# Two directions of a recurrence on different halves of the PSUM partitions

## The chip, the core and the metric

The kernel runs on one core of a Trainium2 chip. The metric is the device time of one execution in microseconds. Three executions of the kernel before took 3052.81, 3056.64 and 3072.35 us, a median of 3056.64 us.

The engines are called by the profile's names: PE is TensorE's matmul unit, PEld its loads of stationary operands, DVE is VectorE, ACT is ScalarE, POOL is GpSimd, SP issues the DMAs.

## The reference

Two layers over 256 context tokens and 256 latent tokens, 1024 channels wide. A layer projects its normalised input with one wide matrix, feeds three token mixers (a bidirectional RWKV-7, a bidirectional gated linear recurrence, a neighbourhood attention), merges them by gates, and ends with a gated MLP. The change touches the RWKV-7 mixer alone, whose heart is this scan, run for 16 heads, forwards and backwards:

```python
def step(S, inp):
    r_t, w_t, k_t, v_t, kk_t, a_t = inp
    sa = jnp.einsum('bhvk,bhk->bhv', S, -kk_t)
    S = (S * w_t[:, :, None, :] + sa[..., None] * (kk_t * a_t)[:, :, None, :]
         + v_t[..., None] * k_t[:, :, None, :])
    return S, jnp.einsum('bhvk,bhk->bhv', S, r_t)
```

S is a 64x64 state for each head. The context goes first, and its last state begins the latent tokens' scan; the outputs of the two directions are added.

## The kernel before, in words

**Layout.** Channels lie on the 128 partitions, the 512 tokens (context, then latent) along the free dimension. The big products (the input projection, tiles `pj`; the MLP, `fg`, `fu`, `fo`; the merges) go through `mm3` (L240): each weight tile is split into a high and a low part (`wh` on ACT, L225; `wl` on DVE or POOL, L228), and three matmuls of 128x128 weights with 512 tokens (256 for latent tokens alone) stand for one product. There are thousands of them, and they fill PE wherever nothing else is due.

**The recurrence in chunks.** A pair of heads takes 128 channels, so a layer has 8 pairs. The scan of a pair is done in 8 chunks of 64 tokens. What lies within a chunk is solved by products and a triangular inverse beforehand: `rw_gram` (L571), `rw_inv` (L632, a chain of some 62 small DVE instructions, tiles `itmp` and `AT`) and `rw_inv2` (L671). What goes from chunk to chunk is `rw_seq` (L697). It has two directions d and two heads h, so every step is four products of 64 output columns, for (d, h) = (0,0), (0,1), (1,0), (1,1), the list `dh`. For each chunk i:

- `r` (L720): G times [state; values], into PSUM partitions 64 to 127. ACT copies all four to `r1` (L724).
- `yp` with `RT` (L726 to L728, through `ymm`, L710): the old state's part of the outputs. Its stationary operand lies on 64 partitions, that of `r` on 128.
- POOL scales the old state by its decay into `sg` (L732).
- `sa` (L735): the inverse times `r1`, into PSUM partitions 0 to 63. ACT copies the four, negated, to SV (L737).
- `sp` (L741): the state's update, into PSUM partitions 0 to 63. DVE adds it to `sg` and writes the next state into SV (L745; L747 where there is no `sg`).
- `yp` with `Gm` (L748 to L750, through L710): the rest of the outputs.

An output product `yp` of chunk c goes to partitions 0 to 63 where c is even and to 64 to 127 where it is odd; the two directions take their chunks in opposite order, so within a step their halves differ.

These products are fp32, and each is two records of LDWEIGHTS and two of MATMUL in the trace: 8 records for a step of four.

**What sets the order.** The program is traced part by part for each pair (the string `order` in the table CFG, L54 and L104; `T` is `rw_seq`), each part with a priority. A list scheduler works out, from the dependences, its own costs and these priorities, the order in which every engine takes its instructions. On the chip each engine keeps to its order, and PE waits at a product whose operand is late even if a projection behind it is ready.

Of the kernel before, what the change touches and what calls it, by code (L numbers as in the profile page):

```python
# [10 lines left out]
F32 = mybir.dt.float32  # L11
F32R = mybir.dt.float32r
AF = mybir.ActivationFunctionType
ALU = mybir.AluOpType
AX = mybir.AxisListType
PSUM = bass.MemoryType.PSUM
# [3 lines left out]
P = 128  # L20
# [31 lines left out]
# per layer: the order in which a head pair's parts are traced, their priorities, how the products of the other  # L52
# mixers are spread beside them, and which engine takes the work that several could take
# [104 lines left out]
class Net:  # L158
# [51 lines left out]
    # ---- weights: raw -> (hi, lo) in float32r  # L210
    def phase(self, l, name, wps=None):
        """From here on the weights rotate among wps; where their low parts are worked out: 1 for GpSimd."""
        self.lo, self.wn = CFG[l]["lo"][name], 0
        if wps:
            self.wps, self.wi = wps, 0
# [49 lines left out]
    # ---- rms statistics of the tokens a ... b - 1: acc holds the sums of squares over the channel tiles  # L265
# [15 lines left out]
    def stat(self, st, sq, a, b, first, last):  # L281
        """Adds the sums of sq over its channels to st, a column for 128 tokens."""
# [13 lines left out]
    # ---- conditioning vectors of a layer: mod[128, 48, 2]  # L296
# [16 lines left out]
    def ada_chunk(self, l, n, kind="c"):  # L313
        """Columns 512 n ... 512 n + 511 of the modulation, four column groups side by side on TensorE."""
# [22 lines left out]
        # modulation: h = x rstd (ng (1 + sc)) + sh ; x += (g ng) o rstd  # L337
# [12 lines left out]
    def layer_consts(self, l):  # L350
# [19 lines left out]
        # softplus(-lam) = max(-lam, 0) + log1p(exp(-|lam|)); log1p(u) = 2 atanh(u / (2 + u))  # L370
# [53 lines left out]
    # ---- A: RWKV-7  # L424
# [16 lines left out]
    def rw_start(self, Q):  # L441
# [4 lines left out]
        # stacked over the partitions: (hi, lo) of w, (lo, hi) of a  # L446
# [14 lines left out]
    def rw_key(self, R, Q, p, n0):  # L461
# [15 lines left out]
        # normalised key  # L477
# [93 lines left out]
    def rw_gram(self, R, u, n0):  # L571
        nc = self.nc
        KR, BK = u["KR"], u["BK"]
        G = R.tile([P, 2, 2, 2, NCH, 64], F32, tag="Gm", name="Gm")  # part, d, h, c
# [22 lines left out]
    def rw_rows(self, R, u, n0):  # L597
# [3 lines left out]
        # from here on [beta; k] decayed to the end of its chunk  # L601
# [3 lines left out]
        # value rows by token, for both directions  # L605
# [12 lines left out]
        # rows by token of [beta; k]  # L618
# [13 lines left out]
    def rw_inv(self, R, u):  # L632
# [9 lines left out]
        if self.cfg['f1']:  # L642
            # the block beside them makes room for the rows of keys
# [10 lines left out]
        # columns s of the inverse: rows 0-63 hold the odd ones, rows 64-127 the even ones, both in the even places  # L654
# [16 lines left out]
    def rw_inv2(self, R, u):  # L671
# [4 lines left out]
        T1 = Ap  # rows 0-31: T11, rows 96-127: Q  # L676
# [20 lines left out]
    def rw_seq(self, R, u, n0):  # L697
# [16 lines left out]
        for i in range(NCH):  # L714
            cs = (i, STEP1[i])
            gcb = gC[:, :, :, i:i + 1].rearrange("p d h o -> p (d h) o").to_broadcast([64, 4, 64])
            S0 = SV[0:64, i].rearrange("p d h v -> p (d h) v")
            pr = self.ps("q", "r1").rearrange("p (x v) -> p x v", v=64)
            for d, h in dh:
                nc.tensor.matmul(pr[64:128, 2 * d + h], lhsT=G[:, 0, d, h, cs[d], :], rhs=SV[:, i, d, h, :],  # L720
                                 start=True, stop=True)
            rs = R.tile([P, 4, 64], F32, tag="r1", name="r1")
            r1 = rs[64:128]
            nc.scalar.activation(r1, pr[64:128, 0:4], AF.Copy)  # L724
# [9 lines left out]
            for d, h in dh:  # L734
                nc.tensor.matmul(pa[0:64, 2 * d + h], lhsT=TT[:, d, h, cs[d], :], rhs=r1[:, 2 * d + h, :],  # L735
                                 start=True, stop=True)
            nc.scalar.activation(S0, pa[0:64, 0:4], AF.Copy, scale=-1.0)  # L737
            if i < NCH - 1:
                pp = self.ps("q", "sp").rearrange("p (x v) -> p x v", v=64)
                for d, h in dh:  # L740
                    nc.tensor.matmul(pp[0:64, 2 * d + h], lhsT=Bt[:, d, cs[d], 64 * h:64 * h + 64],  # L741
                                     rhs=SV[:, i, d, h, :], start=True, stop=True)
                S1 = SV[0:64, i + 1].rearrange("p d h v -> p (d h) v")
                if sg is not None:
                    nc.vector.tensor_tensor(S1, pp[0:64, 0:4], sg, op=ALU.add)  # L745
                else:
                    nc.vector.tensor_copy(S1, pp[0:64, 0:4])  # L747
# [847 lines left out]
```

## Time and profile before

| | |
|---|---|
| times of three runs | 3052.81, 3056.64, 3072.35 us |
| profiled execution: its own time from the first to the last instruction (its span) | 3050.6 us |
| PE busy | 2886.2 us, 95% |
| DVE busy | 1968.9 us, 65% |
| ACT busy | 1411.1 us, 46% |
| POOL busy | 840.6 us, 28% |
| mean granted TensorE clock | 0.959 |

No time of the profiled execution beyond its span is listed. A matmul's end is modelled in this profile: a projection matmul is shown with 0.39 us and the next one starts 0.23 us after it. So what a product costs PE is read from the starts of the matmuls around it, not from busy time.

### The profile page before, as it was taken

What the parts mean: (1) busy time and instruction counts of PE and PEld (TensorE: products, weight loads), DVE (VectorE), ACT (ScalarE), POOL (GpSimd) and SP (SyncE); (2) the same over time, 40 slices, a digit from 0 to 9 for tenths busy, and PEclk for the clock granted to TensorE, in tenths of its full rate; (3) what the DMA queues carried; (4) which work ended last, traced back from release to release, by engine and by line L of the source; (5) the groups of instructions that cost most, each with busy time, mean ns of one, the idle gap of its engine ahead of it and who ended that gap; (6) DMA issues with size and microseconds to landing.
All of it is one profiled execution on the core that took longest, in us unless ns stands there. A gap on an engine that the chain in (4) does not pass through costs nothing. (4 is left out here: it accounts for less than half of the span.)

```text
span 3050.6 us, 53179 instructions
## 1 busy us (share of the span) xinstructions
PE 2886.2 (95%) x21104; PEld 2265.9 (74%) x21104; DVE 1968.9 (65%) x3745; ACT 1411.1 (46%) x2485; POOL 840.6 (28%) x788
## 2 busy tenths in 40 slices
PE   7999999999999999999999998998999999998998
PEld 5666776766767678687778886776776777788898
DVE  6757658576686653465444267788677778775784
ACT  4454455554455452253323245454554545554553
POOL 3341322424234225100000113433432433414220
PEclk9999999999999899998999998998988999999899
DMA  6222122211222225755562352222222122245653
GB/s 229 81 70 67 59 71 66 74 60 56 69 76 70 84 100 180 273 190 180 198 223 92 107 183 82 62 78 69 68 72 69 62 70 78 77 140 205 222 188 115
DMA packets 130553, 344.39 MB, mean 113 GB/s; under 512 B 14720, under 2 KB 41600, under 8 KB 130304
## 3 DMA queue, kind: packets, MB, share of 16 engines
q1 hardware_dynamic: 123392, 334.69, 33.1%
q10 hardware_dynamic: 6912, 6.29, 0.7%
q8 instruction: 166, 2.72, 0.4%
q14 instruction: 83, 0.68, 0.1%
HBM read 301.08 MB, written 25.17 MB: 107 GB/s over the span
## 5 line engine op out<-in xcount | busy, mean ns | idle before, releaser
L225 ACT ACTIVATE wh<-wr 128x1024 fp32r<-128x1024 f32 (+1 forms) x402 | 420.8, 1048 | 581.0 <-PE pj L247 209.1
L248 PE MATMUL pj<-hh,wl 128*128 128x512 f32 (+1 forms) x1440 | 559.0, 389 | 41.4 <-DVE wl L228 40.0
L246 PE MATMUL pj<-hh,wh 128*128 128x512 f32 (+1 forms) x1440 | 569.7, 397 | 5.8 <-ACT gt L1088 3.0
L228 DVE TENSOR_TENSOR wl<-wr,wh 128x1024 fp32r<-128x1024 f32 (+1 forms) x310 | 398.2, 1285 | 266.5 <-ACT wh L225 244.2
L247 PE MATMUL pj<-hl,wh 128*128 128x512 f32 (+1 forms) x1440 | 556.0, 386 | 0.0
L228 POOL TENSOR_TENSOR wl<-wr,wh 128x1024 fp32r<-128x1024 f32 (+1 forms) x92 | 221.1, 2403 | 637.1 <-ACT wh L225 343.6
L248 PEld LDWEIGHTS pj<-hh,wl 128*128 128x128 f32 x1440 | 280.7, 195 | 104.6 <-DVE wl L228 45.7
L246 PEld LDWEIGHTS pj<-hh,wh 128*128 128x128 f32 x1440 | 280.6, 195 | 70.0 <-issue 16.4
L247 PEld LDWEIGHTS pj<-hl,wh 128*128 128x128 f32 x1440 | 280.4, 195 | 55.1 <-issue 13.4
L666 DVE TENSOR_TENSOR AT<-AT,itmp 128x126 f32<-128x126 f32 (+22 forms) x496 | 154.7, 312 | 11.8
L732 POOL TENSOR_TENSOR r<-SV,gC 64x256 f32<-64x256 f32 x96 | 84.2, 877 | 242.0 <-DVE SV L745 139.8
L664 DVE TENSOR_TENSOR itmp<-AT 128x126 f32<-128x126 f32 (+22 forms) x496 | 138.1, 278 | 12.0
L585 PEld LDWEIGHTS gram<-KR,BK 64*128 64x128 f32 x1024 | 116.3, 193 | 27.4 <-ACT Gm L590 14.8
L585 PE MATMUL gram<-KR,BK 64*128 64x128 f32 (+1 forms) x1024 | 131.3, 288 | 4.9 <-ACT Gm L590 4.7
L246 PE MATMUL fo<-fh,wh 128*128 128x256 f32 (+1 forms) x418 | 131.0, 313 | 0.0
L248 PE MATMUL fo<-fh,wl 128*128 128x256 f32 (+1 forms) x418 | 130.7, 313 | 0.0
L247 PE MATMUL fo<-fl,wh 128*128 128x256 f32 (+1 forms) x418 | 130.4, 312 | 0.0
L246 PE MATMUL fu<-hh,wh 128*128 128x256 f32 (+1 forms) x384 | 126.2, 330 | 3.1 <-DVE fgs L1347 2.4
L246 PE MATMUL fg<-hh,wh 128*128 128x256 f32 (+1 forms) x384 | 127.2, 333 | 0.1
L248 PE MATMUL fu<-hh,wl 128*128 128x256 f32 (+1 forms) x384 | 126.4, 330 | 0.8 <-DVE wl L228 0.8
L247 PE MATMUL fg<-hl,wh 128*128 128x256 f32 (+1 forms) x384 | 126.0, 330 | 0.0
L247 PE MATMUL fu<-hl,wh 128*128 128x256 f32 (+1 forms) x384 | 125.8, 328 | 0.0
(344 smaller groups left out, 6481.6 us busy)
## 6 DMA issues: line engine op xcount, KB each, us to landing
wr<-in_w_in SPq DMA_DIRECT2D x180, 512.0 KB, 3.2
aw<-in_ada_w SPq DMA_DIRECT2D x96, 512.0 KB, 4.4
wr<-in_ffn_w_in SPq DMA_DIRECT2D x96, 512.0 KB, 3.4
wr<-in_w_branch SPq DMA_DIRECT2D x48, 512.0 KB, 3.3
wr<-in_ffn_w_out SPq DMA_DIRECT2D x36, 512.0 KB, 3.5
wr<-in_w_out SPq DMA_DIRECT2D x24, 512.0 KB, 4.4
Gm<-KR SPq DMA_DIRECT2D x32, 256.0 KB, 3.6
wr<-in_ffn_w_out SPq DMA_DIRECT2D x18, 384.0 KB, 3.1
```

Of the source, the lines that this page charges most:

```text
L225: nc.scalar.activation(hi, raw, AF.Copy)
L228: eng.tensor_tensor(lo, raw, hi.bitcast(F32), op=ALU.subtract)
L246: nc.tensor.matmul(o, lhsT=a, rhs=xh[k][:, n0:n1], start=(first and k == 0), stop=False)
L247: nc.tensor.matmul(o, lhsT=a, rhs=xl[k][:, n0:n1], start=False, stop=False)
L248: m = nc.tensor.matmul(o, lhsT=b, rhs=xh[k][:, n0:n1], start=False, stop=(last and k == kt - 1))
L585: nc.tensor.matmul(ps[:, i, 0:nx], lhsT=BK[hs, d, c, :], rhs=KR[hs, 0:nx, d, c, :], start=True, stop=True)
L664: eng.tensor_tensor(tmp, Ap[:, q + 1:32, q:q + 1].to_broadcast([P, nt, ns]), Tf[:, q:q + 1, 0:2 * ns:2].to_broadcast([P, nt, ns]), op=ALU. ...
L666: eng.tensor_tensor(Tf[:, q + 1:32, 0:2 * ns:2], Tf[:, q + 1:32, 0:2 * ns:2], tmp, op=ALU.subtract)
L732: nc.gpsimd.tensor_tensor(sg, S0, gcb, op=ALU.mult)
```

## The change

In `rw_seq` alone the four products of each step are written and issued differently. (The rest of the diff takes comments out, which moves the line numbers by a few.)

- The first direction's and the second direction's `r`, `sa` and `sp` go to different halves of the PSUM partitions, and they are issued by `dy`, which alternates the directions: (0,0), (1,0), (0,1), (1,1).
- Each copy out of PSUM covered both directions. Now there are two: ACT copies the first direction's `r` and `sa`, DVE the second's; the update of the state becomes two DVE additions (for the first chunk, one copy on ACT and one on DVE).

```diff
@@ rw_seq
             pr = self.ps("q", "r1").rearrange("p (x v) -> p x v", v=64)
-            for d, h in dh:
-                nc.tensor.matmul(pr[64:128, 2 * d + h], lhsT=G[:, 0, d, h, cs[d], :], rhs=SV[:, i, d, h, :],
-                                 start=True, stop=True)
+            for d, h in dy:
+                nc.tensor.matmul(pr[64 - 64 * d:128 - 64 * d, h], lhsT=G[:, 0, d, h, cs[d], :], rhs=SV[:, i, d, h, :],
+                                 start=True, stop=True, skip_group_check=True)
             rs = R.tile([P, 4, 64], F32, tag="r1", name="r1")
             r1 = rs[64:128]
-            nc.scalar.activation(r1, pr[64:128, 0:4], AF.Copy)
+            nc.scalar.activation(r1[:, 0:2], pr[64:128, 0:2], AF.Copy)
+            nc.vector.tensor_copy(r1[:, 2:4], pr[0:64, 0:2])
...
             pa = self.ps("q", "sa").rearrange("p (x v) -> p x v", v=64)
-            for d, h in dh:
-                nc.tensor.matmul(pa[0:64, 2 * d + h], lhsT=TT[:, d, h, cs[d], :], rhs=r1[:, 2 * d + h, :],
-                                 start=True, stop=True)
-            nc.scalar.activation(S0, pa[0:64, 0:4], AF.Copy, scale=-1.0)
+            for d, h in dy:
+                nc.tensor.matmul(pa[64 * d:64 * d + 64, h], lhsT=TT[:, d, h, cs[d], :], rhs=r1[:, 2 * d + h, :],
+                                 start=True, stop=True, skip_group_check=True)
+            nc.scalar.activation(S0[:, 0:2], pa[0:64, 0:2], AF.Copy, scale=-1.0)
+            nc.vector.tensor_scalar(S0[:, 2:4], pa[64:128, 0:2], -1.0, None, op0=ALU.mult)
             if i < NCH - 1:
                 pp = self.ps("q", "sp").rearrange("p (x v) -> p x v", v=64)
-                for d, h in dh:
-                    nc.tensor.matmul(pp[0:64, 2 * d + h], lhsT=Bt[:, d, cs[d], 64 * h:64 * h + 64],
-                                     rhs=SV[:, i, d, h, :], start=True, stop=True)
+                for d, h in dy:
+                    nc.tensor.matmul(pp[64 * d:64 * d + 64, h], lhsT=Bt[:, d, cs[d], 64 * h:64 * h + 64],
+                                     rhs=SV[:, i, d, h, :], start=True, stop=True, skip_group_check=True)
                 S1 = SV[0:64, i + 1].rearrange("p d h v -> p (d h) v")
-                if sg is not None:
-                    nc.vector.tensor_tensor(S1, pp[0:64, 0:4], sg, op=ALU.add)
-                else:
-                    nc.vector.tensor_copy(S1, pp[0:64, 0:4])
+                for d in range(2):
+                    o, ps = S1[:, 2 * d:2 * d + 2], pp[64 * d:64 * d + 64, 0:2]
+                    if sg is not None:
+                        nc.vector.tensor_tensor(o, ps, sg[:, 2 * d:2 * d + 2], op=ALU.add)
+                    elif d:
+                        nc.vector.tensor_copy(o, ps)
+                    else:
+                        nc.scalar.activation(o, ps, AF.Copy)
```

The scheduler answers with another order. On PE, in one chunk of the first pair of the first layer, the order before is this (L720 is `r`, L735 `sa`, L741 `sp`, L710 the outputs; `x4` is four products in a row):

```order
L246 MATMUL pj_1354<-hh_363,wh 128x512
L720 MATMUL r_1778<-SV,Gm 64x64 x4
L710 MATMUL yp<-SV,RT 64x64 x4
L247 MATMUL pj_1354<-hl_371,wh 128x512
L735 MATMUL sa<-r_1783,RT 64x64 x4
L248 MATMUL pj_1354<-hh_363,wl 128x512
L246 MATMUL pj_1354<-hh_364,wh 128x512
L247 MATMUL pj_1354<-hl_372,wh 128x512
L741 MATMUL sp<-SV,Bt 64x64 x4
L710 MATMUL yp<-SV,Gm 64x64 x4
```

And the same place on PE in the order of the change (L721 is `r`, L737 `sa`, L744 `sp`):

```order
L721 MATMUL r_1759<-SV,Gm 64x64
L710 MATMUL yp<-SV,RT 64x64 x2
L246 MATMUL pj_1354<-hh_363,wh 128x512
L721 MATMUL r_1759<-SV,Gm 64x64 x3
L710 MATMUL yp<-SV,RT 64x64 x2
L247 MATMUL pj_1354<-hl_371,wh 128x512
L737 MATMUL sa<-r_1764,RT 64x64
L248 MATMUL pj_1354<-hh_363,wl 128x512
L737 MATMUL sa<-r_1764,RT 64x64 x3
L246 MATMUL pj_1354<-hh_364,wh 128x512
```

The first direction's first product, whose operand comes from one engine, now stands apart from the three behind it, the first of which takes its operand from a later instruction on DVE, and projections stand between them.

Over the whole program, a stretch of products of `rw_seq` between two other matmuls is called an entry here. PE has 428 entries before and 848 in the change. Of the 368 steps (128 `r`, 128 `sa`, 112 `sp`), 341 have their four products in one row before, and 32 in the change. Inside the entries, a product with 64 operand partitions follows one with 128, or the other way round, 86 times before and 170 times in the change. Of the matmuls ahead of the entries, 338 are those of `mm3` before and 666 in the change.

On DVE the same pair's chunks stand like this before:

```order
L236 TENSOR_TENSOR ll<-lw,lh 128x512
L747 COPY SV<-sp 64x256
L745 TENSOR_TENSOR SV<-sp,r_1699 64x256
L745 TENSOR_TENSOR SV<-sp,r_1727 64x256
L745 TENSOR_TENSOR SV<-sp,r_1755 64x256
L745 TENSOR_TENSOR SV<-sp,r_1783 64x256
```

And in the change (L726 copies `r`, L740 copies `sa`, L750 adds):

```order
L752 COPY SV<-sp 64x128
L726 COPY r_1702<-r_1697 64x128
L740 TENSOR_SCALAR SV<-sa 64x128
L750 TENSOR_TENSOR SV<-sp,r_1702 64x128 x2
L726 COPY r_1733<-r_1728 64x128
L740 TENSOR_SCALAR SV<-sa 64x128
L750 TENSOR_TENSOR SV<-sp,r_1733 64x128 x2
```

A chunk has four instructions on DVE where it had one, and each of the three steps now waits for DVE with its second direction.

## Rows read from the trace of the kernel before

**Rows 1.** The page's head: span; busy time, share and instructions by engine.

```profile
span 3050.6 us, 53179 instructions
PE 2886.2 (95%) x21104; PEld 2265.9 (74%) x21104; DVE 1968.9 (65%) x3745; ACT 1411.1 (46%) x2485; POOL 840.6 (28%) x788
```

**Rows 2.** Busy time by stretch: two recurrences, each followed by the stretch behind it.

```profile
core 0: us, PE busy (x) PEld busy (x) DVE busy (x) ACT busy (x) POOL busy (x), PEclk, DMA share, GB/s
534.00:595.00 61.00, 60.27 (x457) 43.59 (x455) 30.09 (x42) 30.67 (x52) 22.18 (x22) 1.00 0.20 70
595.00:665.00 70.00, 65.63 (x438) 47.38 (x438) 58.99 (x144) 34.91 (x71) 20.28 (x21) 0.95 0.20 60
2137.00:2183.00 46.00, 44.70 (x374) 33.34 (x373) 29.45 (x45) 25.82 (x46) 21.57 (x27) 1.00 0.19 64
2183.00:2249.00 66.00, 61.98 (x451) 49.15 (x450) 56.27 (x124) 33.91 (x62) 19.44 (x20) 0.89 0.26 79
```

**Rows 3.** Busy time: another recurrence; then sums of 16 recurrences, of 14 stretches between.

```profile
2249.00:2298.00 49.00, 48.76 (x357) 35.63 (x356) 29.41 (x48) 24.03 (x44) 21.55 (x25) 0.83 0.15 50
...
sum 824.00, PE 809.76 PEld 587.80 DVE 442.07 ACT 412.71 POOL 317.28; mean PE 50.61 PEld 36.74 DVE 27.63 ACT 25.79 POOL 19.83
...
sum 944.00, PE 880.99 PEld 659.69 DVE 802.92 ACT 475.00 POOL 276.52; mean PE 62.93 PEld 47.12 DVE 57.35 ACT 33.93 POOL 19.75
```

**Rows 4.** Timeline: projections alone on PE (start, length, engine, line).

```profile
1479.78 0.39 PE L248 MATMUL fg<-hh,wl 128*128 128x512 f32 x1
...
1482.07 0.39 PE L246 MATMUL fg<-hh,wh 128*128 128x512 f32 x1
```

**Rows 5.** Timeline, PE: one product alone between projections.

```profile
135.95 0.40 PE L248 MATMUL pj<-hh,wl 128*128 128x512 f32 x1
136.27 0.33 PE L720 MATMUL r<-SV,Gm 128*64 128x64 f32 x2
136.53 0.51 PE L246 MATMUL pj<-hh,wh 128*128 128x512 f32 x1
136.88 0.40 PE L247 MATMUL pj<-hl,wh 128*128 128x512 f32 x1
```

**Rows 6.** Timeline, PE: four products into one half of PSUM, between projections.

```profile
139.87 0.40 PE L248 MATMUL pj<-hh,wl 128*128 128x512 f32 x1
140.19 0.67 PE L735 MATMUL sa<-r,RT 64*64 64x64 f32 x8
140.80 0.50 PE L246 MATMUL pj<-hh,wh 128*128 128x512 f32 x1
141.14 0.40 PE L247 MATMUL pj<-hl,wh 128*128 128x512 f32 x1
```

**Rows 7.** Timeline, PE: four output products, two to each half of PSUM.

```profile
179.28 0.39 PE L248 MATMUL pj<-hh,wl 128*128 128x512 f32 x1
179.60 0.46 PE L710 MATMUL yp<-SV,Gm 128*64 128x64 f32 x8
179.99 0.50 PE L247 MATMUL pj<-hl,wh 128*128 128x512 f32 x1
180.32 0.39 PE L248 MATMUL pj<-hh,wl 128*128 128x512 f32 x1
```

**Rows 8.** Timeline, PE: `r` on 128 partitions, then outputs on 64.

```profile
1076.96 0.40 PE L247 MATMUL pj<-hl,wh 128*128 128x512 f32 x1
1077.28 0.68 PE L720 MATMUL r<-SV,Gm 128*64 128x64 f32 x8
1077.89 0.45 PE L710 MATMUL yp<-SV,RT 64*64 64x64 f32 x8
1078.28 0.50 PE L248 MATMUL pj<-hh,wl 128*128 128x512 f32 x1
1078.62 0.39 PE L246 MATMUL pj<-hh,wh 128*128 128x512 f32 x1
```

**Rows 9.** One line's instructions (`r`, L720), and what PE waited for ahead.

```profile
L720 PE MATMUL r<-SV,Gm x1024: 222/222/369, 136.3 to 2726.1; 128*64 128x64 f32 x171
...
  DVE SV L745: 31.2, 34
  issue: 18.3, 54
  DVE SV L747: 2.9, 8
```

**Rows 10.** The same for `sa` (L735).

```profile
L735 PE MATMUL sa<-r,RT x1024: 218/218/367, 140.2 to 2727.6; 64*64 64x64 f32 x171
...
  issue: 15.1, 51
  ACT r L724: 11.3, 38
```

**Rows 11.** Groups by line and form, DVE: busy, mean ns | idle before.

```profile
L745 DVE TENSOR_TENSOR SV<-sp,r 64x256 f32<-64x256 f32 x96 | 39.8, 414 | 115.7 <-PE sp L741 115.1
L1039 DVE SCALAR_TENSOR_TENSOR s<-bias,s 128x128 f32<-128x128 f32 x64 | 18.4, 289 | 9.4 <-PE s L1037 8.0 <-ACT wh L225 0.3 <-ACT pr L902 0.2
L747 DVE COPY SV<-sp 64x256 f32<-64x256 f32 x16 | 6.7, 416 | 53.6 <-PE sp L741 53.6
```

**Rows 12.** One line's instructions (`sp`, L741): durations as min, median, max.

```profile
L741 PE MATMUL sp<-SV,Bt x896: 222/222/370, 142.2 to 2724.5; 128*64 128x64 f32 x180
```

## The prediction

> **What bounds the kernel now.** I read the page's head first [rows 1]: PE is busy for 95% of the span and DVE for 65%. Since a matmul's end is modelled there, I then read the stretches. In a recurrence of the first layer PE is busy 60.27 of 61 us and DVE 30.09; in the stretch behind it PE 65.63 and DVE 58.99 of 70. In the second layer it is the same, 44.70 and 29.45 of 46, then 61.98 and 56.27 of 66 [rows 2]. Over all 16 recurrences PE is busy 809.76 of 824 us, over 14 stretches between them 880.99 of 944 with DVE at 802.92 [rows 3]. So where the changed code runs, PE sets the pace, and DVE has room there and little elsewhere. What a piece of the recurrence costs is therefore the time it takes from PE's stream of projections.
>
> That time is read from starts. Ten projections in a row take 1482.07 - 1479.78 = 2.29 us, 0.229 each [rows 4]. From here on a cost is the time from the start of the projection ahead of an entry to the start of the second projection behind it, less 2 x 0.229.
> - One product alone, two records: 136.88 - 135.95 - 0.458 = 0.472 us [rows 5].
> - Four into one half, eight records: 141.14 - 139.87 - 0.458 = 0.812 [rows 6].
> - Four with two in each half: 180.32 - 179.28 - 0.458 = 0.582 [rows 7].
>
> Six more records on one half cost 0.340 us, 0.0567 each, so the entry itself costs 0.472 - 2 x 0.0567 = 0.359, before any product. Four records on each half would by that cost 0.359 + 4 x 0.0567 = 0.586, and [rows 7] have 0.582: **the two halves run beside each other, and only the fuller half counts**. Behind `r`, outputs whose operands lie on 64 partitions add 1.202 - 0.812 = 0.390 [rows 8, 6]. Four records on a half are 0.227 of it, and 0.163 is left for the change from 128 to 64 operand partitions.
>
> **The change part by part.** The edit halves the products' time where a step's four stand together. The order on PE shows that they mostly no longer do: 848 entries in place of 428, because the second direction's operand comes from a later instruction on DVE and the scheduler puts projections in between.
> - **Entries:** 420 more x 0.359 = +150.8 us.
> - **Products:** a step of four took 8 x 0.0567 = 0.454. Split one and three it takes 0.113 + 0.227 (of the three, two are the second direction's and fill its half), which saves 0.113. Some 320 of the 368 steps: -36.3. The 32 that still stand together and some 16 split two and two save 0.227: -10.9. Together -47.2. The counts of records say the same: two for each product, 1024 for `r` and `sa` and 896 for `sp` [rows 9, 10, 12].
> - **Changes of operand partitions inside entries:** 84 more x 0.163 = +13.7.
> - **Outputs:** in the first layer a step's output products are now issued by direction, so that each pair fills one half: with `RT`, 7 chunks x 8 pairs x 0.227 = +12.7. Those with `Gm` stand behind `sp`, which leaves a half free: before, the fuller half had 8 + 4 records; split, the two entries have on average 5 and 7, so nothing.
> - **Waits for DVE:** PE stood idle ahead of `r` for 31.2 us in 34 cases and 2.9 in 8 until DVE had written the state [rows 9]. Entries with no such wait show idle time too, 18.3 us in 54 and 15.1 in 51 [rows 9, 10], 0.32 each, which the price of an entry holds already. So the waits proper are 34.1 - 42 x 0.32 = 20.7 us for 112 steps. `sa` and `sp` now depend on DVE in the same way. The bounds are nothing (the first direction's product and a projection stand ahead and give DVE time) and 2 x 20.7 = 41.4; I take 20, the middle, since one of these covers is there nearly always and is about as long as a DVE instruction.
> - **DVE's own time:** 128 + 128 + 2 x 96 + 16 = 464 instructions of 64x128. No such row exists; a 128x128 one out of PSUM takes 289 ns, and the 64x256 ones that go took 414 and 416 [rows 11]. 464 x 0.289 - 96 x 0.414 - 16 x 0.416 = +87.7 us. I cost it at nothing: DVE is busy 442 of 824 us in the recurrences [rows 3]. Were that cover gone, it would cost up to 88 us. It could not gain, as DVE gets more instructions. What queues behind a DVE copy that waits for PE are mostly the weights' low parts (`wl`), for which projections wait.
> - **ACT's halved copies, SP, POOL:** ACT has shorter copies on a path that PE covers: nothing. No DMA and no POOL instruction is added; POOL's product now waits for the later of two additions, and a whole chunk's steps stand between it and its use: nothing.
>
> Sum: 150.8 - 47.2 + 13.7 + 12.7 + 20 = +150 us on the profiled execution's 3050.6 [rows 1], 3200.6. The median of the runs, 3056.64, stands 6.0 above that span, so I expect 3207 us, 4.9% more.
>
> [...]
>
> **The rivals.**
> 1. *Twice the pace at no price: faster.* If an additional entry fell into time in which PE now waits, only the pace would show. Every step would save 0.227, 368 x 0.227 = 84 us: 2973 us. For it: the pace of [rows 7]. Against it: a lone product with no wait ahead still costs 0.472 [rows 5], and PE is busy 98% of the recurrences [rows 3]. It decides below 84 / 420 = 0.20 us for an entry. Chance 0.05. [...]
> 2. *Gain and price cancel: within 1%.* The stretches between the recurrences have 944 - 881 = 63 us of idle PE [rows 3]. If the projections that recurrences no longer need went there, and a third of the new entries (those beside other small products) were free, the sum would be 150 - 63 - 50 = 37, which gives 3094; with no waits for DVE 3074. Chance 0.04. Against it: DVE is busy 85% of those stretches, so they do not shorten with PE's share.
> 3. *DVE becomes the bound.* All 41 us of waits and half of the 88 come on the path: 3207 + 21 + 44 = 3272. For it: four DVE instructions for a chunk each stand at the queue's head until PE is there, and DVE already idles 115.7 and 53.6 us ahead of its additions [rows 11]. Against it: DVE is half idle in these stretches. Chance 0.14.
> 4. *The clock.* One recurrence had a granted clock of 0.83 and took 49 us where its like took 46 [rows 2, 3]. If thinner work on PE did that to all 16: 16 x 3 = 48 us, 3255. Chance 0.05.
> 5. *The change does not do what it says*: `r`, `sa` and `sp` do not run beside each other on two halves. Then the 47 us are not saved: 3254. The products of [rows 7], with operands of the same shape as `r` and `sp`, speak against it. Chance 0.02.
>
> **How the numbers follow.** The forecast has 0.70. A measurement of this kernel can tell about 1% from no change; slower by more than that are the forecast and rivals 3 to 5, 0.91; within it rival 2, 0.04; faster rival 1, 0.05. The range: downwards, the 92 new entries that do not follow a projection of `mm3` (420 - (666 - 338)) may be free, 33 us, the waits may be nothing, 20, and half of the 63 us of idle PE may be used: 3207 - 33 - 20 - 30, about 3125. Upwards it takes in rivals 4 and 5 and most of rival 3: 3285.
>
> **What would show it.** In the changed kernel's trace, a lone `r` or `sa` should again cost 0.47 us and a row of three 0.59 rather than 0.69; four over both halves 0.58. The recurrences should be longer by about 9 us each (150 / 16) and the stretches between them as long as before. PE's idle time ahead of `sa` should be put down to DVE copies in about half its cases, where it was ACT. I am wrong if lone entries cost under 0.2 us, if the stretches between shrink by as much as the recurrences grow, or if DVE's lateness rather than the entries makes the sum.

## The result, and the profile after

The changed kernel took 3358.42 us (median of four runs, 3347.00 to 3371.80) against 3056.56 us for the kernel before on the same chip: a ratio of 1.0966, interval 1.0925 to 1.1008. It is slower, as forecast, but by 302 us where 150 were forecast, and 73 us above the upper end of the range.

The page's head of the changed kernel answers to [rows 1]; the third line is the clock that TensorE was granted in 40 slices of the span, in tenths:

```profile
span 3345.2 us, 53467 instructions
PE 3128.2 (94%) x21104; PEld 2368.4 (71%) x21104; DVE 2011.9 (60%) x4097; ACT 1393.5 (42%) x2501; POOL 817.8 (24%) x788
...
PEclk9999999999999899989999987887967789859899
```

PE is as busy as before, 94% of a longer span. New is the last third of the clock's line: sevens, a six and a five. The mean clock is 0.912, before it was 0.959. The traces of the two kernels hold two levels of the granted clock, 1.00 and 0.50 (stretches at each stand below), so a mean clock of c over a stretch of t us means that 2 (1 - c) t of them ran at the lower level, which I call half-clock time. Over the span that is 2 x 0.041 x 3050.6 = 250 us before and 2 x 0.088 x 3345.2 = 589 us after. If PE were the bound throughout and all of its work took twice as long at the lower level, a microsecond there would do half a microsecond's work. By that estimate the 339 us more are worth at most some 170 us; the rows at both levels below show 1.6 and 1.78 times as long, not twice.

To see where, I cut the program by layers, from the first `r` of a layer's first pair to the first `r` of its last pair. The kernel before, busy time by stretch, layer 0 and then layer 1 (the columns of [rows 2]; the mean clock, PEclk, is the first number behind POOL's):

```profile
core 0: us, PE busy (x) PEld busy (x) DVE busy (x) ACT busy (x) POOL busy (x), PEclk, DMA share, GB/s
136.30:1053.90 917.60, 888.57 (x6240) 633.91 (x6239) 613.10 (x1303) 448.71 (x842) 287.77 (x291) 0.97 0.21 68
1920.70:2684.70 764.00, 716.06 (x5630) 548.87 (x5629) 586.87 (x1160) 394.99 (x719) 283.46 (x299) 0.94 0.22 71
```

The changed kernel, the same two stretches:

```profile
137.20:1155.70 1018.50, 981.14 (x6273) 661.85 (x6272) 645.61 (x1457) 444.29 (x856) 292.13 (x292) 0.96 0.20 63
2028.70:2980.60 951.90, 863.06 (x5735) 625.56 (x5734) 604.00 (x1356) 398.19 (x754) 265.04 (x303) 0.80 0.19 60
```

Layer 0 grew by 101 us at nearly the same clock. Layer 1 grew by 188 us, though it has only 139 of the 420 new entries (340 where it had 201; layer 0 has 508 where it had 227), and its clock fell from 0.94 to 0.80: half-clock time 92 us before, 381 after. (The stretch also holds 105 more of PE's instructions; at its mean of 764.0 / 5630 us each, an estimate, that is some 14 us of the 188.) The rest of the program is within 6 us of before.

The changed kernel's recurrences by stretch: two neighbours of layer 1 with 49 and 48 entries, and the sum of all 16, which answers to [rows 3]:

```profile
2563.00:2632.00 69.00, 67.61 (x406) 44.71 (x406) 33.70 (x71) 24.40 (x52) 18.11 (x21) 0.69 0.15 46
2722.00:2775.00 53.00, 52.29 (x388) 34.01 (x386) 23.13 (x60) 19.01 (x44) 12.33 (x16) 0.94 0.15 43
...
sum 1093.00, PE 1075.82 PEld 695.26 DVE 555.58 ACT 435.33 POOL 291.36; mean PE 67.24 PEld 43.45 DVE 34.72 ACT 27.21 POOL 18.21
```

The recurrences took 1093 us where they took 824, 17 each and not 9. PE is busy 98% of them as before, and DVE half of them. The two neighbours, nearly alike in work, took 69 and 53 us: the longer had a clock of 0.69, the shorter one of 0.94.

What one entry costs, on PE's timeline of the changed kernel (start, length), at the full clock:

```profile
140.31 0.40 PE L247 MATMUL pj<-hl,wh 128*128 128x512 f32 x1
140.63 0.33 PE L737 MATMUL sa<-r,RT 64*64 64x64 f32 x2
140.89 0.50 PE L248 MATMUL pj<-hh,wl 128*128 128x512 f32 x1
141.22 0.40 PE L246 MATMUL pj<-hh,wh 128*128 128x512 f32 x1
...
141.93 0.39 PE L246 MATMUL pj<-hh,wh 128*128 128x512 f32 x1
142.25 0.44 PE L737 MATMUL sa<-r,RT 64*64 64x64 f32 x6
142.62 0.50 PE L247 MATMUL pj<-hl,wh 128*128 128x512 f32 x1
142.96 0.39 PE L248 MATMUL pj<-hh,wl 128*128 128x512 f32 x1
```

The lone `sa` costs 141.22 - 140.31 - 0.458 = 0.452 us (0.47 was forecast) and the row of three 142.96 - 141.93 - 0.458 = 0.572 (0.59 was forecast; 0.69 would have been three on one half). The same view inside the slow recurrence of layer 1, where the projections have 256 columns:

```profile
2569.28 0.41 PE L248 MATMUL pj<-hh,wl 128*128 128x256 f32 x1
...
2570.77 0.41 PE L246 MATMUL pj<-hh,wh 128*128 128x256 f32 x1
2571.11 0.69 PE L737 MATMUL sa<-r,RT 64*64 64x64 f32 x6
2571.73 0.58 PE L247 MATMUL pj<-hl,wh 128*128 128x256 f32 x1
2572.11 0.41 PE L248 MATMUL pj<-hh,wl 128*128 128x256 f32 x1
...
2734.77 0.28 PE L248 MATMUL pj<-hh,wl 128*128 128x256 f32 x1
2734.89 0.28 PE L246 MATMUL pj<-hh,wh 128*128 128x256 f32 x1
```

At the lower clock seven projections take 2570.77 - 2569.28 = 1.49 us, 0.213 each; in the neighbour at the full clock two start 0.12 apart. And the row of three costs 2572.11 - 2570.77 - 0.426 = 0.914 us instead of 0.572. No idle time is shown ahead of any of these products: PE works without a pause, the projections at 0.56 of their pace (0.12 / 0.213) and the entry at 0.63 (0.572 / 0.914). So by these rows a microsecond at the lower level costs 0.44 us in projections and 0.37 in an entry, somewhat less than half.

What PE did before the clock fell differs from case to case. The lower clock of the longer recurrence consists of two low stretches, of which the first begins ahead of it, behind a wait of 2.58 us for DVE; the second begins within it, where PE had waited no more than 0.5 us at a time. PE's timeline at the wait, then the two low stretches (columns of [rows 2], a clock of 0.50):

```profile
2550.36 0.36 PE L246 MATMUL pj<-hh,wh 128*128 128x256 f32 x1 [2.58 <-DVE v L431]
...
2550.70:2584.80 34.10, 31.05 (x213) 21.22 (x211) 20.91 (x27) 11.65 (x22) 11.64 (x14) 0.50 0.22 66
2601.90:2622.40 20.50, 20.50 (x107) 14.52 (x107) 6.83 (x19) 4.99 (x12) 1.25 (x2) 0.50 0.16 49
```

In the kernel before, in the recurrence at 0.83 of [rows 3], the clock fell with no idle time shown at all: PE is busy for 30.70 us in a row at the full clock, and the lower level follows.

```profile
2252.10:2282.80 30.70, 30.70 (x257) 23.28 (x257) 19.03 (x32) 17.61 (x32) 15.64 (x17) 1.00 0.17 60
2282.80:2296.50 13.70, 13.46 (x73) 8.83 (x72) 9.15 (x16) 3.87 (x7) 5.91 (x9) 0.50 0.13 41
```

The clock fell little more often in layer 1 than before, 17 times and 13, but it stayed low for 22 us on average where it was 7.

For layer 1 half of the additional half-clock time, the estimate above, is (381 - 92) / 2 = 145 us; with the 0.37 to 0.44 of the rows at both levels it is 107 to 127. Beside the entries, 188 - 139 x 0.359 = 138 are left, which lies between the two.

The waits for DVE, forecast at 20 us. What ended PE's idle time ahead of `sa` (us, times) in the changed kernel, the line that answers to [rows 10]:

```profile
L737 PE MATMUL sa<-r,RT x1024: 216/218/367, 140.6 to 3035.2; 64*64 64x64 f32 x171
...
  issue: 44.5, 136
  ACT r L725: 15.5, 34
...
  DVE r L726: 1.0, 2
```

Forecast was that about half the cases would be put down to DVE's copies. It is 2 cases and 1.0 us. "issue" grew with the number of entries, 0.33 us a case, which their price holds already. The rows of DVE itself:

```profile
L750 DVE TENSOR_TENSOR SV<-sp,r 64x128 f32<-64x128 f32 x192 | 55.3, 288 | 100.0 <-PE sp L744 96.5
L740 DVE TENSOR_SCALAR SV<-sa 64x128 f32<-64x128 f32 x128 | 37.5, 293 | 99.2 <-ACT SV L739 97.1 <-POOL sw L977 0.6
L726 DVE COPY r<-r 64x128 f32<-64x128 f32 x128 | 36.4, 284 | 133.7 <-ACT r L725 132.0
```

Their lengths, 284 to 293 ns, are the 289 of the forecast. What they wait for was not forecast: **DVE's copy of the second direction does not wait for PE but for ACT's copy of the first.** The two read different halves of one PSUM tile, and the program lets one follow the other. So the second direction comes an ACT copy later (272 to 276 ns; where DVE stood idle for it, at 585.94 us, its copy began 0.03 us behind the end of ACT's), and the scheduler, which knows of that order, fills the time with projections: that is where the 1 + 3 splits would come from, which experiment 7 puts to the test.

### The profile page after: what moved, and what is told of

Same layout as the page of the kernel before. It is cut to its first block, busy times and chain, and to the rows that moved or that the text cites. A ratio compares the mean times of both kernels' runs of the same rounds, so it can differ in the third digit from the quotient of the medians.

```text
span 3345.2 us, 53467 instructions
## 1 busy us (share of the span) xinstructions
PE 3128.2 (94%) x21104; PEld 2368.4 (71%) x21104; DVE 2011.9 (60%) x4097; ACT 1393.5 (42%) x2501; POOL 817.8 (24%) x788
## 5 line engine op out<-in xcount | busy, mean ns | idle before, releaser
L246 PE MATMUL pj<-hh,wh 128*128 128x512 f32 (+1 forms) x1440 | 590.5, 412 | 33.2 <-DVE k L431 13.3
L248 PE MATMUL pj<-hh,wl 128*128 128x512 f32 (+1 forms) x1440 | 582.6, 406 | 15.5 <-DVE wl L228 14.1
L247 PE MATMUL pj<-hl,wh 128*128 128x512 f32 (+1 forms) x1440 | 584.1, 406 | 0.0
L246 PEld LDWEIGHTS pj<-hh,wh 128*128 128x128 f32 x1440 | 292.0, 203 | 100.6 <-issue 39.0
L247 PEld LDWEIGHTS pj<-hl,wh 128*128 128x128 f32 x1440 | 292.5, 203 | 55.3 <-issue 10.1
L734 POOL TENSOR_TENSOR r<-SV,gC 64x256 f32<-64x256 f32 x96 | 107.4, 1118 | 420.0 <-DVE SV L750 262.9
L585 PE MATMUL gram<-KR,BK 64*128 64x128 f32 (+1 forms) x1024 | 149.1, 312 | 9.1 <-ACT Gm L590 8.7
L585 PEld LDWEIGHTS gram<-KR,BK 64*128 64x128 f32 x1024 | 131.5, 214 | 36.2 <-ACT Gm L590 15.7
L666 DVE TENSOR_TENSOR AT<-AT,itmp 128x126 f32<-128x126 f32 (+22 forms) x496 | 144.2, 291 | 10.4
L721 PEld LDWEIGHTS r<-SV,Gm 128*64 128x64 f32 x1024 | 71.9, 148 | 78.8 <-issue 47.1
L248 PE MATMUL fg<-hh,wl 128*128 128x256 f32 (+1 forms) x384 | 126.4, 330 | 0.3 <-DVE wl L228 0.3
```

The lines of the kernel that those rows point to most:

```text
L246: nc.tensor.matmul(o, lhsT=a, rhs=xh[k][:, n0:n1], start=(first and k == 0), stop=False)
L247: nc.tensor.matmul(o, lhsT=a, rhs=xl[k][:, n0:n1], start=False, stop=False)
L248: m = nc.tensor.matmul(o, lhsT=b, rhs=xh[k][:, n0:n1], start=False, stop=(last and k == kt - 1))
L585: nc.tensor.matmul(ps[:, i, 0:nx], lhsT=BK[hs, d, c, :], rhs=KR[hs, 0:nx, d, c, :], start=True, stop=True)
L666: eng.tensor_tensor(Tf[:, q + 1:32, 0:2 * ns:2], Tf[:, q + 1:32, 0:2 * ns:2], tmp, op=ALU.subtract)
L721: nc.tensor.matmul(pr[64 - 64 * d:128 - 64 * d, h], lhsT=G[:, 0, d, h, cs[d], :], rhs=SV[:, i, d, h, :], start=True, stop=True, skip_group ...
```

## The experiments

Two theories stood at the start. **Entries**: the sum of the forecast holds and some of its rows are too low, in both layers alike. **Clock**: the entries cost what was forecast, and layer 1, whose projections are narrower, falls to the lower clock when they are cut up further. A third, **serial copies**, asks why there are 848 entries at all. Each experiment's entries are those on PE in layer 0 and layer 1; before they are 227 and 201, after 508 and 340.

### 1 and 2. The change in one layer alone

```diff
+        (self.rw_seq_new if self.l == 0 else self.rw_seq_old)(R, u, n0)   # 1: layer 0 changed; 2: with l == 1
```

> The first layer's recurrences are written as in the change, the second layer's as before; PE has 709 entries, all 281 new ones in the first layer. Theory 'entries' (each new entry costs 0.36 us at full clock): 281 x 0.36 = 101 us less some 25 for the products' pace plus about 25 for the outputs, some 3157 us, with a granted clock near that of the kernel before (0.96). Theory 'clock' (the rest of the change's 302 us is a lower granted clock in the second layer) expects the same. Theory 'serial copies' (DVE's copy waits for ACT's in every step, and the longer chain of a chunk is what costs) expects both layers to share the loss: 150 us here, 3207 us.

> The second layer's recurrences as in the change, the first layer's as before; 567 entries, 139 new ones. 'Entries' alone: 139 x 0.36 = 50 us, some 3100 us at an unchanged clock. 'Clock': the granted clock of the second layer's stretches falls to about 0.80 from 0.94, and the time is 3057 + 190 = 3247 us. 'Serial copies': 3207 us, with PE idle ahead of sa and sp and the clock lower only where PE is idle.

Layer 0 alone (508 and 201 entries): 3162.97 us, before 3052.83, ratio 1.0362 [1.0326, 1.0399], 110 us more. Layer 1 alone (227 and 340): 3261.07, ratio 1.0681 [1.0632, 1.0730], 208 us more. Together 318, close to the 302 of both at once, so the two parts do not need each other. Layer 1 of the second kernel, by stretch:

```profile
1930.20:2906.40 976.20, 896.71 (x5737) 649.91 (x5736) 603.22 (x1355) 399.07 (x754) 267.16 (x303) 0.77 0.18 58
```

With twice the new entries layer 0 costs half as much. Its 281 bring 0.39 us each; the 139 of layer 1 bring 1.50 each, at a clock of 0.77. The clock theory had both runs, the entries alone missed the second by 160 us, and the serial copies missed both, by some 50 us either way.

### 3. The copies split, all products on one half

The products of the kernel before, into one half, but copied and added by direction as in the change:

```diff
-            nc.scalar.activation(r1, pr[64:128, 0:4], AF.Copy)
+            nc.scalar.activation(r1[:, 0:2], pr[64:128, 0:2], AF.Copy)
+            nc.vector.tensor_copy(r1[:, 2:4], pr[64:128, 2:4])
...
```

> The products are as before (one half of PSUM, both heads of a direction in a row); only the copies are split by direction between ACT and DVE. 829 entries. 'Entries': the split copies alone make the entries and the loss; without the pace of two halves it is as slow as the change or slower, 401 x 0.36 = 144 plus whatever the clock adds: 3200 at an unchanged clock, 3350 to 3400 with the clock of the change. If it were the halves or the alternation that cost, it would stand near 3057.

3465.93 us, ratio 1.1335 [1.1284, 1.1386]: slower than the change by 107 us and than the 3350 to 3400 expected, with nearly as many entries (467 and 362). Its layer 1:

```profile
2052.50:3074.70 1022.20, 947.04 (x5656) 688.08 (x5655) 589.61 (x1321) 392.53 (x738) 252.68 (x298) 0.75 0.17 53
```

So the split copies alone, without the halves, make a loss of 413 us, and the halves, with the alternating order that came with them, take some of it back.

### 4. One tile, the products of a step kept together

The second direction's product, whose operand is late, is issued first; the other three are ordered behind it.

```diff
+        dz = [(d, h) for h in range(2) for d in (1, 0)]
...
-            for d, h in dy:
-                nc.tensor.matmul(pr[64 - 64 * d:128 - 64 * d, h], ...)
+            g1 = together(dz, ...)   # the first product, then the others with tc.issue_after(first)
```

> The change with the second direction's first product issued first in every step and the step's others queued behind it on PE, so that the four stand together: 322 of 368 steps in one row, 566 entries. 'Entries': 138 x 0.36 = 50 us more, 322 x 0.227 = 73 us less, some 3035 us, with the clock of the kernel before. 'Serial copies': the chain of a chunk is still longer by a DVE copy behind an ACT copy in each step, PE waits, and it stays above 3150 us.

3226.47 us, ratio 1.0555 [1.0498, 1.0611], with 385 and 181 entries. The entries theory had 3035 and missed by 190; 'serial copies' had over 3150 with PE waiting, and that came. The entries were those counted (322 of the 368 steps stood in a row of four; in layer 0 the outputs stood apart from them). What that sum lacked lies in layer 1: with fewer entries than before it is 131 us longer, at a low clock:

```profile
1979.20:2874.60 895.40, 777.75 (x5735) 588.00 (x5734) 615.13 (x1356) 396.36 (x754) 269.43 (x303) 0.82 0.20 64
```

PE is busy 87% of it, where it is 91% of layer 1 in the changed kernel: here PE does wait for the later direction, 8.2 us ahead of `sp`, 5.5 ahead of `r` and 5.1 ahead of `sa` until DVE is done, and it is idle for 118 us of the layer in all, where it was 48 before.

### 5 and 6. Denser projections in layer 1, before and changed

In layer 1 three projections work on the 256 latent tokens alone. Here they run over all 512; the additional columns are used by nothing. This is more work for PE, in matmuls of 512 columns.

```diff
-        self.shift(self.proj(p, n0), p, r, n0)
+        self.shift(self.proj(p), p, r, n0)
-        pg = self.proj(34 + ct, n0)
+        pg = self.proj(34 + ct)
-        pq = self.proj(42 + p, n0)
+        pq = self.proj(42 + p)
```

> The kernel before, but three projections of each pair of the second layer (r, the second recurrence's gate, the attention's queries) are computed for all 512 tokens in place of 256; the additional columns are not used. 8 x 3 x 24 matmuls that are 0.115 us longer: 66 us if PE bounds the second layer throughout, less where DVE does; the granted clock as before or a little higher. Both theories: 3057 + 30 to 66 = 3090 to 3120 us.

> The same three wider projections in the changed kernel: more full-width work on PE in the second layer, everything else as in the change. 'Clock' (the second layer lost 145 us to a clock that falls because PE's work is thin there): the clock of the second layer rises, and the 66 us of additional work cost clearly less than in the kernel before or even save time: 3300 to 3370 us, a distance of 200 to 250 from dense_before in place of 302. 'Serial copies and waits' (the lower clock is only a companion): the distance stays 302 us, some 3400 us.

The kernel before took 3172.39 us with it, ratio 1.0374 [1.0358, 1.0389], 114 us more than without, where 30 to 66 were expected; where the rest comes from was not followed up. The changed kernel took 3309.94 (its profiled run, the slowest, 3345.86), ratio 1.0847 [1.0790, 1.0903]: **48 us less than without the additional work** (on another chip; against the kernel before on the same chip the ratio is 1.0847 where it was 1.0966, and the intervals do not overlap). The distance between the two fell from 302 us to 138, more than the 200 to 250 expected. Layer 1 of the denser kernel before, then of the denser changed kernel with one of its recurrences, which now has the full clock:

```profile
1927.70:2798.90 871.20, 803.95 (x5648) 599.52 (x5647) 591.94 (x1161) 394.61 (x721) 263.05 (x296) 0.92 0.21 63
```

```profile
2057.00:2956.90 899.90, 847.39 (x5636) 599.17 (x5635) 610.57 (x1312) 382.50 (x727) 264.97 (x296) 0.90 0.20 60
...
2450.00:2510.00 60.00, 58.70 (x412) 38.47 (x410) 36.96 (x83) 25.72 (x53) 22.16 (x28) 1.00 0.18 54
```

The changed kernel's clock in layer 1 rose from 0.80 to 0.90, though it has even more entries there than without (370 against 340). In that layer the changed kernel is now 29 us behind and not 188. PE also waited less there, 53 us where it was 89. But waits alone do not account for it: PE's busy time itself fell, from 863.06 to 847.39 us, though it had more to do, which shorter waits cannot bring about. Its half-clock time went from 381 us to 180, in 16 low stretches for 17, and shorter ones. That the clock is the missing term is shown by this pair.

### 7 and 8. A PSUM tile for each direction

```diff
-            pr = self.ps("q", "r1").rearrange("p (x v) -> p x v", v=64)
+            pr = [self.ps("q", "r1").rearrange("p (x v) -> p x v", v=64) for _ in range(2)]
...
+            nc.vector.tensor_copy(r1[:, 2:4], pr[1][0:64, 0:2])
```

Kernel 7 is the change with this edit for `r`, `sa` and `sp`; kernel 8 is kernel 4 with it.

> The change with a PSUM tile of its own for each direction in r, sa and sp, so that DVE's copy need not wait for ACT's. 582 entries, 106 steps in one row, most others two and two by direction. 'Entries': 154 x 0.36 = 55 us more than before, some 24 us less for the pace: 3090 us at an unchanged clock, and about 3150 with half of the clock loss of the change. 'Serial copies': with the copies side by side DVE's waits for ACT ahead of its copies go, and the time is near that of the kernel before or under it.

> Both: the four products of a step queued together and a PSUM tile for each direction. 528 entries. 'Entries': 100 x 0.36 = 36 us more, up to 60 us less for the pace: some 3035 us at an unchanged clock. The run before this one with the products together alone missed its 3035 by 190 us and had a low clock in the second layer; if the serial copies were the reason, this one reaches 3035 to 3080; if not, it stays above 3150 with a clock near 0.92.

Kernel 7 took 3153.58 us, ratio 1.0305 [1.0288, 1.0322], with 311 and 271 entries; kernel 8 took 3114.67, ratio 1.0183 [1.0160, 1.0207], with 303 and 225. DVE's waits in the changed kernel (waiter, what it waited for, us, times, longest):

```profile
DVE r L726 <- ACT r L725: 132.0, 89, 4.7
DVE SV L740 <- ACT SV L739: 97.1, 81, 3.5
```

and in kernel 7:

```profile
DVE r L726 <- PE r L721: 170.8, 92, 11.7
DVE SV L740 <- PE sa L737: 80.8, 83, 5.1
```

With tiles of their own both copies wait mainly for PE, and the scheduler makes 582 entries of 848. So the serial copies were worth 266 entries and, with a clock in layer 1 of 0.91 for 0.80, 205 us: the largest part of the loss. That is the 3150 of 'entries' with half of the clock's loss; 'serial copies' had hoped for the kernel before or less. Kernel 8 lies between its two forecasts, 3080 at most and 3150 at least. The order between the two reads of one tile stands in the program; whether the chip needs it was not shown, since no run has two such reads of one tile without it.

### 9 and 10. Rows of four by priority

Kernels 4 and 8, with the products behind the first at the highest priority, the outputs too, so that nothing comes between:

```diff
-                    with self.tc.issue_after(first.ins):
+                    with self.tc.issue_after(first.ins), self.tc.high_priority(offset=100000):
                         f(d, h)
```

> As the run with the four products queued together (one PSUM tile for both directions, DVE's copy behind ACT's), but the products behind the first have the highest priority, so that no projection comes between: 381 entries, 353 of 368 steps in one row. 'Entries' at an unchanged clock: 47 x 0.36 = 17 us less than before and 353 x 0.227 = 80 us less for the pace, 2960 us. 'Clock': the second layer's loss stays as long as PE's work there is as thin as it was with the products together: 2960 + 60 to 120 = 3020 to 3080. 'Serial copies': the chain of a chunk, not PE, sets the recurrences, and it stays near 3226.

> The same priorities with a PSUM tile for each direction, so that the two copies run side by side: 449 entries, some 162 steps in one row by the names and as many in two rows that follow each other. 'Entries': 21 x 0.36 = 8 us more, about 60 us less for the pace: 3005 us at an unchanged clock. 'Clock': 3005 + 40 to 70. 'Serial copies': clearly under the run with one tile, and under the kernel before.

With one tile: 3135.20 us, ratio 1.0271 [1.0236, 1.0305], 200 and 181 entries, 353 rows of four. With two: 3125.36, ratio 1.0232 [1.0195, 1.0270], 224 and 225. One tile by stretch, layer 0 and layer 1:

```profile
136.90:1042.80 905.90, 864.50 (x6275) 609.25 (x6274) 661.74 (x1458) 437.68 (x857) 281.52 (x292) 0.95 0.22 71
1887.10:2775.10 888.00, 769.80 (x5735) 585.52 (x5734) 616.32 (x1356) 396.81 (x754) 269.49 (x303) 0.83 0.20 65
```

And two tiles:

```profile
142.10:1091.50 949.40, 894.98 (x6275) 629.85 (x6274) 677.36 (x1457) 441.61 (x856) 272.78 (x291) 0.94 0.20 67
1943.70:2742.50 798.80, 737.58 (x5642) 564.18 (x5641) 621.14 (x1321) 386.85 (x732) 261.63 (x300) 0.89 0.21 69
```

Both runs missed all their forecasts, by 50 us and more. With one tile layer 0 is now 12 us below before (917.60). Layer 1 is 124 above with 20 entries fewer than before: its clock stays at 0.83. The totals of the two differ by only 10 us, with intervals that overlap, but by layers they are far apart: with two tiles layer 0 is 43 us longer, and layer 1 is 89 us shorter, at a clock of 0.89, with PE idle for 61 us of it and not 118. (Some 90 of PE's instructions moved out of that stretch with two tiles; outside both stretches the kernel with two tiles is 33 us longer.) So in layer 1 the order of the copies still counts when the rows stand together, by the waits that it leaves and by the clock; kernels 4 and 8 show the same.

### 11 and 12. Rows of four in layer 0 only, on two halves and on one

Both leave layer 1 as it was before. In layer 0 kernel 11 is kernel 9; kernel 12 has the same priorities, with the products of the kernel before on one half and one copy for both directions.

```diff
+        (self.rw_seq_new if self.l == 0 else self.rw_seq_old)(R, u, n0)
+            g1 = together(dh, lambda d, h: nc.tensor.matmul(pr[64:128, 2 * d + h], ...))   # kernel 12 only
```

> The first layer as in the run with rows of four and one PSUM tile, the second layer as in the kernel before; 401 entries, 27 fewer than before. 'Entries' and pace: 27 x 0.36 = 10 us and some 180 x 0.227 = 41 us less; the second layer and its clock as before: 3010 to 3030 us, faster than before. If the two halves give nothing in the end (serial copies eat the pace), it stands at 3045 like its partner without the halves.

> The same priorities in the first layer for the products and copies of the kernel before (one half of PSUM, one copy for both directions): 401 entries as well. 'Entries': 10 us less than before, 3045 us. What its partner is faster than this one is the pace of the two halves, less what the second copy costs.

Kernel 11 took **3031.03 us against 3057.94, ratio 0.9901 [0.9878, 0.9924]: 1% faster than the kernel before**, 1 us above its forecast. Kernel 12 took 3076.97, ratio 1.0069 [1.0044, 1.0094], 32 us over its forecast. Both have 200 and 201 entries. Layer 0 of kernel 11, then of kernel 12:

```profile
137.20:1040.90 903.70, 862.54 (x6273) 607.98 (x6272) 662.34 (x1458) 437.80 (x857) 281.38 (x292) 0.95 0.22 71
```

```profile
135.70:1086.80 951.10, 914.85 (x6274) 645.52 (x6273) 603.58 (x1303) 450.70 (x849) 299.56 (x292) 0.96 0.21 67
```

At equal entries the two halves, with the split copies that come with them, are worth 46 us in one layer; 180 steps at 0.227 would be 41. Against the kernel before, kernel 11 gains only 27 us, of which 27 fewer entries would be 10: the priorities themselves cost something, which kernel 12 shows alone. In this layer it is 33 us longer than the kernel before (917.60) with 27 entries fewer, and PE is busy for 26 us more; some 7 us of that are 32 more projections in the stretch, and the clock is 0.96 for 0.97. Why was not followed up.

### Layer 1 over all variants

For each kernel: how much longer layer 1 is than before (764.0 us), half of its additional half-clock time by 2 (1 - c) t (an estimate that takes the levels 1.00 and 0.50 for all of them), what is left, and its additional entries at 0.359. The clock has two digits, so half the half-clock time is good to some 5 us, and by the rows at both levels, 1.6 and 1.78 times as long, it is rather too high.

| kernel | longer | clock | half of half-clock time | left | entries x 0.359 |
|---|---|---|---|---|---|
| the change | +188 | 0.80 | 145 | 43 | +50 |
| 2, layer 1 alone | +212 | 0.77 | 179 | 33 | +50 |
| 3, copies split | +258 | 0.75 | 210 | 48 | +58 |
| 4, together | +131 | 0.82 | 115 | 16 | -7 |
| 7, two tiles | +59 | 0.91 | 28 | 31 | +25 |
| 8, together, two tiles | +55 | 0.86 | 69 | -14 | +9 |
| 9, rows, one tile | +124 | 0.83 | 105 | 19 | -7 |
| 10, rows, two tiles | +35 | 0.89 | 42 | -7 | +9 |

The two terms give all eight to within 26 us, and the clock is the larger in every row but that of kernel 7, where the two are alike. The three kernels with two tiles lost 35 to 59 us in this layer, the five with one tile 124 to 258. The table is an account and not a proof: the two terms do not tell what holds the clock low.

## Why the prediction was right in its direction and wrong in its size

- **What bounds the kernel**: right. PE stays busy 98% of the recurrences, and DVE is half idle there.
- **Entries, 420 x 0.359 = 150.8, and the products' pace, -47.2**: right in price. The lone `sa` cost 0.452 and the row of three 0.572. Changed alone, layer 0 made the kernel 110 us slower, where its forecast from the same terms was 101; and in the changed kernel, at 0.96 for 0.97, it grew by 101. Kernels 11 and 12, alike but for the halves and the split copies, differ by 46 us where the pace gives 41.
- **Changes of operand partitions and outputs, 13.7 and 12.7**: not measured by themselves. What the terms above leave over has room for them.
- **Waits for DVE, 20 us**: too high, about 1 us ahead of `sa` and 0.9 ahead of `sp`; for the first of a step, `r`, 12.9 us in 40 cases, which is less than before [rows 9]. The second direction is late, but the scheduler knew it and paid in entries instead, which the count from the order already held. "In about half its cases" failed.
- **DVE's own 88 us, hidden**: right. The copies and additions took 284 to 293 ns, and DVE's busy time rose by only 43 us, since others of its instructions became shorter (the 32 scans of L522 took 1.43 us each where they took 1.86, and 48 of L666, 128x126, 320 ns where they took 557). Rival 3 did not come.
- **The clock**: this is the step that failed. The sum took all its prices from rows at the full clock, and nothing in it stood for the clock; rival 4 put the clock at "16 x 3 = 48 us", with a chance of 0.05. By half of the half-clock time, an estimate, it cost some 145 us in layer 1 and 170 over the span; by the 0.37 to 0.44 of the rows at both levels, 107 to 127 and 125 to 149. Without it, 3345.2 - 170 = 3175 to 3345.2 - 125 = 3220 us of span stand on either side of the 3200.6 of the sum. The 3 us came from one recurrence at 0.83, which I took as the worst that could come. It was a mild case beside those of the changed kernel's layer 1, where one recurrence had 0.63 (2428 to 2493 us). Both of the low clocks in the forecast's own rows (0.89 in [rows 2] and 0.83 in [rows 3]) are from layer 1, many of whose projections have 256 columns. And I priced the recurrences alone; of layer 1's 381 us at the lower clock nearly half, some 174, lie in the stretches behind them.
- **"The recurrences longer by about 9 us each and the stretches between them as long as before"**: 17 us each, and the stretches between, 944 us before, took 992: 82 us more in layer 1, at a lower clock, and 34 less in layer 0.
- **Why the operands come apart**: I took the 848 entries as given. That one copy waits for the other, and that this and not the two engines as such makes most of the splits, was shown by kernel 7 only.

What stays open: what keeps the clock of layer 1 low. With its products cut up and put between narrow projections, 340 entries for 201, the clock stood at 0.80 for 0.94 and stayed low for 22 us on average for 7; with wider projections it stood at 0.90. But kernels 4 and 9 have a low clock, 0.82 and 0.83, with no more entries than before, and longer waits, 118 us of idle PE in the layer for 48; and the changed kernel has both, thinner work and 89 us of idle PE. No run tells the thinner work and the waits apart there. Every edit also gave another order on all engines, so no run changes one thing alone.

## What to carry to other kernels

Before pricing an edit from rows at the full clock, look at the clock of each stretch that it touches: layer 1, which showed 0.94, fell to 0.80 when its products were cut up, and at the lower level the price of an entry of three products grew by more than half, from 0.572 us to 0.914. When one tile is read in parts by two engines, see whether one read waits for the other, and give each part its own tile: in layer 1 every kernel with split copies and two tiles lost less than every one with one, 35 to 59 us against 124 to 258. Two halves of PSUM paid where the products that share them stood in one row: 46 us in a layer against the same priorities without them, and 27 against the kernel before. Look at the layers, too, and not only at the total: two kernels within 10 us of each other differed by 89 in one layer and by 43 the other way in another.

## What the runs showed of the hardware that was not expected

- TensorE's clock fell to its lower level where the profile shows no pause of PE: before, at 2282.8 us, behind 30.70 us in which it was busy throughout. And work did not bring it back at once: in the change it stayed low for 34.1 us in which PE was busy 31.05, and for 20.5 us in which it was busy all the time.
- More work on PE made the program faster: 3358.42 us to 3309.94, a ratio to the kernel before of 1.0847 for 1.0966, with layer 1's clock going from 0.80 to 0.90.
- An entry of three products cost 0.572 us at the full clock and 0.914 at the lower one, and projections of 256 columns 0.12 and 0.213: both kept more than half of their pace, 0.63 and 0.56.
